# Norm, transposes and raw blocks of the first tokens set inside the preceding A22 products, first pieces in step, operands in another order

## The chip, the cores and the metric

The kernel runs on one core of a Trainium2 chip. The metric is the device time of one execution in microseconds (us). TensorE (PE) multiplies, VectorE (DVE), ScalarE (ACT) and GpSimd (POOL) do the elementwise work, and SyncE (SP) issues most DMAs.

## The reference

A trunk of two layers on x of 1 x 1024 x 1024 in float32. Cut to what matters here:

```python
def sq_relu_mlp(h, w_in, w_out):
    return jnp.square(jax.nn.relu(h @ w_in)) @ w_out

for layer in range(2):
    if layer == 0:
        x = x + rwkv7_time_mix(rmsnorm(x, rwkv_norm_g[0]), ...)   # ends in "@ w_o"
    else:
        x = x + fox_layer(rmsnorm(x, attn_norm_g[0]), w_q, ..., w_o, k_sh, v_sh, c_sh)
    x = x + sq_relu_mlp(rmsnorm(x, mlp_norm_g[layer]), w_in[layer], w_out[layer])
    if layer == 0:
        k_sh, v_sh, c_sh = shared_kv(x, kv_norm_g, kv_w, ...)     # rmsnorm(x) @ kv_w
```

w_in is 1024 x 4096, w_out 4096 x 1024, w_q and w_o 1024 x 1024, kv_w 1024 x 2064. Each large product thus begins with an RMS norm of the residual stream, which the product before it has just finished.

## The kernel before

**Products.** A float32 number is split into a high part `h` (rounded by a cast) and a low part `l` (the rest), and a product is three passes: hh, lh and hl. `split` makes the two parts with one cast and one subtraction. Large products use a scheme of seven products on the four quarters of each matrix: A11, A12, A21, A22 are the quarters of the left one, B11 to B22 those of the right one; S1 to S4 are sums on the left, T1 to T4 (code: `t1` to `t4`) sums on the right. The seven products are A11 B11, A12 B21, S1 T1, S2 T2, S3 T3, S4 B22 and A22 T4, and their sums give the four quarters of the result.

**Operands.** The normed x has to stand transposed on the right side of `mlp_in` and `stage_qkv` (q, k, v). `norm_T` scales four row tiles of x (128 x 1024 each; the first half is the first 512 tokens) by their `rstd`, and 32 transposes of 128x128 on PE bring them into PSUM; `emit_raw` copies them to SBUF as raw blocks, B11 and B21 from the first half, B12 and B22 from the second. `operands` then forms t1 to t4 and splits all of them: tiles `xh..`, `xl..` with the operand's name (xhB, xlB of B11, B21, B22; xhT, xlT of T1 to T4). The tables `ENG["m0"]`, `ENG["m1"]`, `ENG["q"]` give for each instruction a letter of the engine: v for DVE, s for ACT, p for POOL.

**Stages**, in order: mixing and recurrence of layer 0 with its w_o (to 874 us), `mlp_in` of layer 0 (16 pairs; `products(pr)` runs the seven products of one pair, 12 matmuls of 128x512 each; to about 1205), `mlp_out` of layer 0 (ends in its A22 product, 192 matmuls, to 1519), `stage_qkv` (six groups by `proj_seven`, each product 48 matmuls of 128x256; to about 1840), attention, w_o by `add_product` (to 2179), `mlp_in` of layer 1 (to about 2520) and `mlp_out` of layer 1.

**Where products and operands meet.** In `mlp_in` of layer 0 the raw blocks of the first half are made early, in the recurrence; the first two pairs' A11 and A12 stand, by a generator that stops there (`yield`), before the second transposes; afterwards each pair runs in `IN_ORDER`, the first at a higher priority. In `mlp_in` of layer 1 and `stage_qkv` `operands` begins with the first norm and transposes itself, behind the end of the product before; in q/k/v a group's A11 stands before the second transposes.

**What sets the order.** A scheduler with a simulated timeline fixes the instruction order of every engine beforehand; engines take their queues strictly in order. `tc.high_priority` moves work forward, and matmuls issued by `k.pe` keep the program's order on PE. Memory pools are opened and closed in a stack; a tile that takes the place of another waits for its last reader.

## Time and profile before

| | us |
|---|---|
| median of 3 runs | 2847.68 (2845.11 to 2850.22) |
| profiled execution, its own time | 2847.68 |
| its span | 2845.9 |
| busy: PE / DVE / ACT / POOL | 2605.9 / 2071.9 / 1282.4 / 799.2 |
| mean granted clock of PE | 0.951 |

The profiled execution is the median run; its span is 1.8 us shorter than its time. Busy is the sum over the instructions of an engine. PE's matmuls overlap in their ends, so what a stretch could have taken is read from the number of its matmuls and the distance of their starts. A wait is given with the engine and line that ended it. Granted clock 1.00 is the upper of PE's two levels (2.4 GHz), 0.50 the lower (1.2 GHz).

### The profile page before, as it was taken

To read this page: it belongs to the slowest core of one execution; us is meant where nothing else is said; L and a number is where in the kernel's file an instruction comes from. 1 tells how busy PE (TensorE), PEld (TensorE's weight loads), DVE (VectorE), ACT (ScalarE), POOL (GpSimd) and SP (SyncE) were. 2 spreads that over 40 slices of the span, in tenths; PEclk is the share of its full clock that TensorE was granted. 3 is DMA by queue.
4 is the path that set the end of the run, shared out by engine and by line. 5 is a ranking of instruction groups with operands and counts; after the bars stand their busy time and mean duration, and the time that the engine had idled before them with its cause. 6 is when DMAs were issued, how large, how long until landed. Compare 5 with 4: busy or idle time off the path is not lost. (4 is left out here: it accounts for less than half of the span.)

```text
span 2845.9 us, 46112 instructions
## 1 busy us (share of the span) xinstructions
PE 2605.9 (92%) x17922; PEld 2180.6 (77%) x17922; DVE 2071.9 (73%) x3275; ACT 1282.4 (45%) x2215; POOL 799.2 (28%) x575
## 2 busy tenths in 40 slices
PE   7998788789998999999997899899987899999999
PEld 4777677577776888788886899877876688878887
DVE  7049998777777777747776878577789877755675
ACT  6354443332234555534343434377745455543332
POOL 3056453375655000000304322233356200000030
PEclk9999889889998999999998899999998999999999
DMA  3358674565431444467561232455430344466764
GB/s 119 133 182 243 169 213 125 169 175 146 124 76 37 163 163 155 170 216 258 192 223 60 69 110 76 146 151 144 111 134 1 96 155 156 139 228 218 242 196 139
DMA packets 382315, 428.49 MB, mean 151 GB/s; under 512 B 139696, under 2 KB 259744, under 8 KB 382096
## 3 DMA queue, kind: packets, MB, share of 16 engines
q1 hardware_dynamic: 379088, 417.08, 47.0%
q0 software_dynamic: 3008, 8.47, 0.8%
q8 instruction: 141, 2.31, 0.4%
q14 instruction: 78, 0.64, 0.1%
HBM read 295.31 MB, written 130.15 MB: 150 GB/s over the span
## 5 line engine op out<-in xcount | busy, mean ns | idle before, releaser
L356 PE MATMUL mm<-oh 128*128 128x512 f32 x896 | 351.3, 392 | 9.9 <-ACT oh L702 9.9
L356 PE MATMUL mm<-ol,oh 128*128 128x512 f32 x896 | 351.3, 392 | 1.7 <-DVE ol L705 1.7
L356 PE MATMUL mm<-oh,ol 128*128 128x512 f32 x896 | 350.7, 391 | 0.0
L702 ACT CAST oh<-ra 128x1024 fp32r<-128x1024 f32 x112 | 117.8, 1054 | 354.7 <-PE mm L356 257.1
L705 DVE TENSOR_TENSOR ol<-ra,oh 128x1024 fp32r<-128x1024 f32 x112 | 142.7, 1276 | 140.5 <-ACT oh L702 140.3
L739 PE MATMUL mm<-xlT,ah 128*128 128x512 f32 x512 | 203.1, 397 | 13.1 <-DVE xlT L705 13.1
L738 PE MATMUL mm<-xhT,ah 128*128 128x512 f32 x512 | 202.5, 396 | 12.4 <-DVE xhT L704 6.4
L356 PEld LDWEIGHTS mm<-oh 128*128 128x128 f32 x896 | 169.7, 189 | 46.0 <-ACT oh L702 10.7
L356 PEld LDWEIGHTS mm<-ol,oh 128*128 128x128 f32 x896 | 169.5, 189 | 38.3 <-DVE ol L705 2.7
L740 PE MATMUL mm<-xhT,al 128*128 128x512 f32 x512 | 197.2, 395 | 0.2 <-DVE al L705 0.2
L356 PEld LDWEIGHTS mm<-oh,ol 128*128 128x128 f32 x896 | 169.6, 189 | 35.2
L702 ACT CAST ah<-w 128x512 fp32r<-128x512 f32 x125 | 77.6, 622 | 157.1 <-PE mm L739 150.3
L738 PE MATMUL mm<-xhB,ah 128*128 128x512 f32 x368 | 144.9, 394 | 0.0
L739 PE MATMUL mm<-xlB,ah 128*128 128x512 f32 x368 | 144.6, 393 | 0.0
L740 PE MATMUL mm<-xhB,al 128*128 128x512 f32 x368 | 144.5, 393 | 0.0
L1485 POOL DMA_DIRECT2D d_x<-xt x16 | 8.8, 549 | 482.7 <-DVE xt L1478 482.3
L1485 POOL DMA_DIRECT2D out_dram<-xt x16 | 8.7, 545 | 477.3 <-DVE xt L1478 477.0
L739 PEld LDWEIGHTS mm<-xlT,ah 128*128 128x128 f32 x512 | 97.8, 191 | 36.7 <-DVE xlT L705 16.4
L705 DVE TENSOR_TENSOR ol<-rb,oh 128x1024 fp32r<-128x1024 f32 x96 | 125.6, 1310 | 0.0
L738 PEld LDWEIGHTS mm<-xhT,ah 128*128 128x128 f32 x512 | 97.7, 191 | 35.3 <-ACT xhT L702 11.8
L356 PE MATMUL mm<-wl,xhT 128*128 128x256 f32 x384 | 111.2, 289 | 7.9 <-POOL wl L705 7.9
L356 PE MATMUL mm<-wh,xlT 128*128 128x256 f32 x384 | 111.7, 291 | 6.6 <-POOL xlT L705 6.6
(528 smaller groups left out, 7481.6 us busy)
## 6 DMA issues: line engine op xcount, KB each, us to landing
rb<-in_mlp_w_out_dram SPq DMA_DIRECT2D x128, 512.0 KB
ra<-d_H SPq DMA_DIRECT2D x112, 512.0 KB
w<-in_mlp_w_in_dram SPq DMA_DIRECT2D x64, 512.0 KB
d_H<-z SPq DMA_DIRECT2D x32, 1024.0 KB
d_H<-sums SPq DMA_DIRECT2D x32, 512.0 KB
raw<-in_rwkv_w_rkv_dram SPq DMA_DIRECT2D x24, 512.0 KB
d_KR<-KR SPq DMA_DIRECT2D x16, 512.0 KB
KRz<-d_KR SPq DMA_DIRECT2D x16, 512.0 KB
```

What stands on the lines that cost most here:

```text
L356: return self.tc.keep_in_program_order(self.tc.nc.tensor.matmul(*args, **kw))
L702: nc.scalar.copy(hi, src)
L705: lo_eng.tensor_tensor(lo, src, hi.bitcast(F32), op=ALU.subtract)
L738: te.matmul(out, ah, bh, start=i == 0, stop=False)
L739: te.matmul(out, ah, bl, start=False, stop=False)
L740: te.matmul(out, al, bh, start=False, stop=i == n - 1)
L1485: nc.gpsimd.dma_start(out[i * P:i * P + P, (D1, D2)[h]], d)
```

## The change

1. `operands` always gets the first half's raw blocks, made earlier by `first_half`, and a list of callbacks, `steps`, between which it makes T1 and T2 (with the second transposes), T3, B22 and T4, in this order; before, T2 came first, then T1, T4, B22, T3. t1 to t4 are written in place.
2. The first two pairs of `mlp_in` run in step, product by product in `START_ORDER`, in the pinned order of PE: A11 and A12 of pair 0, the second transposes, A11 and A12 of pair 1, S1 of both, S2 of both, and so on. Their weights' sums and splits no longer follow letters but stand on DVE and ACT. The three sums go into one tile (`bufs=1`), and an early pair needs one more addition.
3. In `mlp_out` of layer 0 a callback `mid` runs halfway through the A22 product: norm, 32 transposes and raw copies of the first half for q/k/v.
4. In `add_product` (w_o of layer 1) `mid` runs before A22: the same for `mlp_in` of layer 1. The right side's split tiles have 3 buffers, not 4.
5. In q/k/v A11 and A12 of the first group stand before the second transposes, and the pool of the weights is opened before that of the operands.

The diff, cut to this (`early` in `products` means the first two pairs; what passes `raw` and `mid` on to the stages is left out):

```diff
+    for kt in range(NK):
+        b = ("B11", "B21")[kt // 4]
+        parts(b, kt % 4, raw[kt % 4][b], (eng["Bh"][kt], eng["Bl"][kt]))
+    steps[0](X)
+
+    emit = emit_raw(k, raw, lambda b, i: tile_("T4", {"B12": "h", "B22": "l"}[b], i), gcol, eng)
     def second_parts(kt, half, tp):
         i, b = emit(kt, half, tp)
-        if b == "B22":
-            minus("t1", i, "B12", "B11", tile_("T4", "h", i))
-            minus("t2", i, "B22", "t1", tile_("B22", "h", i))
-            parts("T2", i, "t2")
-    if early:
-        for kt in range(NK):
-            first_parts(kt, 0)
-    else:
-        norm_T(k, ps_tile, xt, first_parts, lambda i: [tile_of(i)], eng, 0)
-    if mid is not None:
-        mid(X)
-    if early:
-        ss = pools["B22"].tile([P, 1], F32, name="ss")
-        row_squares(k, xt[NK - 1], last_junk, ss)
-        rsqrt_small(k, pools["B22"], k.rstd[NK - 1], ss, 1.0 / D, 1e-6)
+        r = raw[i]
+        if b == "B12":
+            minus("t1", i, r["B11"], r["B12"], r["B11"])
+            parts("T1", i, r["B11"])
+        else:
+            r["t2"] = tile_("T3", "h", i)
+            minus("t2", i, r["t2"], r["B22"], r["B11"])
+            parts("T2", i, r["t2"])
     norm_T(k, ps_tile, xt, second_parts, lambda i: [tile_("T2", "h", i - 4), tile_("B22", "l", i - 4)], eng, 1)
+    if rows_done is not None:
+        rows_done()
+    steps[1]()
     for i in R4:
-        parts("T1", i, "t1")
-    if after is not None:
-        after()
+        r = raw[i]
+        minus("t4", i, r["B21"], r["B21"], r["t2"])
+        minus("t3", i, r["B12"], r["B22"], r["B12"])
+        parts("T3", i, r["B12"])
+    steps[2]()
     for i in R4:
-        minus("t4", i, "B21", "t2", tile_("B22", "l", i))
-        minus("t3", i, "B22", "B12", t3(i))
-        parts("T4", i, "t4")
+        parts("B22", i, raw[i]["B22"])
+    steps[3]()
     for i in R4:
-        parts("B22", i, "B22")
-        parts("T3", i, "t3")
+        parts("T4", i, raw[i]["B21"])
+    steps[4]()
     return X
...
+def first_half(k, xt, raw, gcol, eng, pool, hn, ps_tile):
...
+    norm_T(k, ps_tile, xt, emit_raw(k, raw, place, gcol, eng), hn, eng, 0)
...
+START_ORDER = ["A11", "A12", "S1", "S2", "S3", "S4", "A22"]
...
-            def part(name, q, src=None):
+                nc.vector.tensor_tensor(A[dst], A[x], A[y], op=op)
+
+            def part(name, src=None):
                 S[name] = [wp.tile([P, NK // 2, P], F32R, tag=t, name=t, bufs=3) for t in ("ah", "al")]
-                es = [eng["wh"][7 * pr + q], eng["wl"][7 * pr + q]] if pr < 2 else ["s", "v"]
-                split(k, None, A[src or name], None, *(engine(k, e) for e in es), dst=S[name])
+                split(k, None, A[src or name], None, nc.scalar, nc.vector, dst=S[name])
...
-            for q, an in enumerate(IN_ORDER):
+            for an in START_ORDER if early else IN_ORDER:
...
-                    k.pe if early and pr < AHEAD and q < 2 else nc.tensor)
+                mm3(k, o, [((ah[:, i], al[:, i]), X[bn][i]) for i in range(NK // 2)], k.pe if early else nc.tensor)
...
+                    if early:
+                        yield
...
                     add(C11, U, o)
                     square(C11)
                 elif an == "S2":
                     add(U, U, o)
+                    if early:
+                        add(V, V, o)
                 elif an == "S1":
-                    V = hp.tile([P, 512], F32, tag="V", name="V", bufs=1)
                     add(V, U, o)
                 elif an == "S3":
-                    add(C22, V, o)
+                    if early:
+                        o22 = o
+                    else:
...
+                    if early:
+                        yield
+                        if pr == 0:
+                            second_place = z(1)
+                        H2 = second_place[:, pr]
+                        add(H2[:, T2], V, o22)
+                        square(H2[:, T2])
+                    C21, C22 = H2[:, T1], H2[:, T2]
...
-                    sums = [hp.tile([P, 2, 512], F32, tag="sums", name="sums") for _ in range(2)]
-                    (S1, S2), S4 = (sums[0][:, i] for i in range(2)), sums[1][:, 0]
+                    sums = hp.tile([P, 3, 512], F32, tag="sums", name="sums", bufs=1)
...
+                if early and an in ("S1", "S2", "S3"):
+                    yield
...
-        X.update(x)
+            next(gens[0])
+            if k.last_row:
+                k.last_row(hp.tile([P, 3, 512], F32, tag="sums", name="sums", bufs=1).rearrange("p a b -> p (a b)")[:, :D],
+                           xp["B22"])
+
+        def both(n):
+            for _ in range(n):
+                for g in gens[:AHEAD]:
+                    next(g)
+
+        def second():
+            next(gens[1])
+            both(1)
+        X.update(operands(k, xp, ps, xt, k.col[f"mlp_norm_g{l}"], eng, raw,
+                          [first, second, lambda: both(1), lambda: both(1), lambda: both(2)]))
         for g in gens:
...
+            if an == "A22":
+                mid(lambda i: [pool.tile([P, 512], F32, tag=t, name="hn", bufs=4) for t in ("S3", "T3")])
...
-                    h_ = op_.tile([P, 512], F32R, tag="h" + side, name="oh", bufs=4)
-                    l_ = op_.tile([P, 512], F32R, tag="l" + side, name="ol", bufs=4)
+                    h_, l_ = (op_.tile([P, 512], F32R, tag=t + side, name="o" + t, bufs=4 if side == "a" else 3) for t in "hl")
                     es = [engine(k, letters[at + side + y][4 * q + i]) for y in "hl"]
...
-        U, V = ([p["k"].tile([P, 512], F32, name=f"{n}{i}") for i in range(4)] for n in "UV")
+        UV = [p["k"].tile([P, 2, 512], F32, name=f"UV{i}") for i in range(4)]
+        U, V = ([t[:, i] for t in UV] for i in range(2))
...
+                if mid is not None and names == ("A22",) and q == KP // 2:
+                    tps = [ps.tile([P, 512], F32, tag="mm", name="tp") for _ in range(4)]
+                    mid([t.rearrange("p a b -> p (a b)") for t in UV], tps)
...
+        if number == 0 and an == "A12":
+            yield
...
+        p1 = ctx.enter_context(tc.tile_pool(name="q_1", bufs=2, reuse_waits="tile"))
         xp = operand_pools(k, ctx, "B11 B22 B21 T1 T2 T3 T4")
-        p1 = ctx.enter_context(tc.tile_pool(name="q_1", bufs=2, reuse_waits="tile"))
...
-        def first_product(x):
...
-            next(groups[0])
...
-            return t3[-1][:, i % 2]
+            step(2)
+
+        def step(n):
+            for _ in range(n):
+                next(groups[0])
...
-        operands(k, xp, ps, xt, None, t3_tile,
-                 lambda i: p1.tile([P, D], F32, tag=("wh", "wl")[i % 2], name="hn"), ENG["q"], first_product, rows_done)
+        X.update(operands(k, xp, ps, xt, None, ENG["q"], raw,
+                          [first, lambda: step(3), lambda: step(1), lambda: None, lambda: step(2)], rows_done))
```

**DVE at the end of `mlp_out` of layer 0 and the start of q/k/v.** xt is the residual, SS the sums of squares, hn (after: UV) the normed rows, w, wl the weights and their low part. Before:

```order
L1478 TENSOR_TENSOR xt_6865<-xt_6865,mm 128x512
L1478 TENSOR_TENSOR xt_7145<-xt_7145,mm 128x512
L92 TENSOR_SCALAR hn<-xt_5233,rstd_75 128x1024
...
L751 TENSOR_TENSOR SS_13683<-SS_13683 128x4
...
L92 TENSOR_SCALAR xhT_14272<-xt_6314,rstd_76 128x512
...
L704 CAST xhB_14167<-xlT_14165 128x512
L92 TENSOR_SCALAR w<-w,cols_419 128x512
L704 CAST xhB_14123<-xlT_14121 128x512
...
L704 CAST xhB_14156<-xlT_14154 128x512
L705 TENSOR_TENSOR xlB_14124<-xlT_14121,xhB_14123 128x512
L705 TENSOR_TENSOR wl<-w,wh 128x1024
```

After (xhB_14116 is a part of B21, xhB_14100 a part of B11; the xt row is the last addition of A22):

```order
L82 TENSOR_SCALAR UV_11819<-xt_5233,rstd_75 128x1024
...
L696 TENSOR_TENSOR ol<-ra,oh 128x1024
...
L695 CAST xhB_14116<-raw 128x512
L696 TENSOR_TENSOR xlB_14117<-raw,xhB_14116 128x512
...
L1500 TENSOR_TENSOR xt_7145<-xt_7145,mm 128x512
L742 TENSOR_TENSOR SS_13625<-SS_13625 128x4
...
L82 TENSOR_SCALAR xhT_14254<-xt_6314,rstd_76 128x512
...
L695 CAST xhB_14100<-raw 128x512
L696 TENSOR_TENSOR xlB_14101<-raw,xhB_14100 128x512
L82 TENSOR_SCALAR w<-w,cols_419 128x512 x6
L696 TENSOR_TENSOR wl<-w,wh 128x1024
```

The first half's norms, and B21's casts, have moved ahead of A22's last additions; B11's casts, the scaling of w and the first wl stand behind the norms of the second half, as before.

**PE at the A22 product of w_o in layer 1.** mm are products, tp the transposes; z (after: hn) holds the normed first half. Before, A22's last matmuls, the first transposes and the second ones:

```order
L1350 MATMUL mm<-oh 128x512
L1350 MATMUL mm<-oh 128x512
L1351 MATMUL mm<-ol,oh 128x512
L1352 MATMUL mm<-oh,ol 128x512
L359 MATMUL tp<-ident,z 128x128 x32
L359 MATMUL tp<-ident,xhT_21741 128x128
```

After, the last matmuls of S4, the first transposes, and A22:

```order
L1369 MATMUL mm<-ol,oh 128x512
L1370 MATMUL mm<-oh,ol 128x512
L349 MATMUL tp<-ident,hn 128x128 x32
L1368 MATMUL mm<-oh 128x512
L1369 MATMUL mm<-ol,oh 128x512
L1370 MATMUL mm<-oh,ol 128x512
```

The 32 transposes stood behind A22's 48 matmuls and stand ahead of them now.

**DVE at the start of `mlp_in` of layer 0**, from the last residual addition's neighbour on: al is the low part of a weight's split, S and w are sums of weights. Before, with the first al here further below:

```order
L586 TENSOR_TENSOR xt_7145<-xt_7145,wo 128x512
L705 TENSOR_TENSOR xlB_9138<-raw,xhB_9137 128x512
L705 TENSOR_TENSOR xlB_9146<-raw,xhB_9145 128x512
L1192 TENSOR_TENSOR S<-w_9155 128x512
L705 TENSOR_TENSOR xlB_9150<-raw,xhB_9149 128x512
L1192 TENSOR_TENSOR w_9155<-w_9153,w_9155 128x512
L101 TENSOR_SCALAR rs_v<-ss 128x1
...
L92 TENSOR_SCALAR xlB_9257<-xt_7145,rstd_76 128x512
L705 TENSOR_TENSOR al<-w_9193,ah 128x512
```

After:

```order
L576 TENSOR_TENSOR xt_7145<-xt_7145,wo 128x512
L696 TENSOR_TENSOR xlB_9137<-raw,xhB_9136 128x512
L696 TENSOR_TENSOR xlB_9145<-raw,xhB_9144 128x512
L1185 TENSOR_TENSOR S<-w_9154 128x512
L696 TENSOR_TENSOR xlB_9149<-raw,xhB_9148 128x512
L696 TENSOR_TENSOR al<-w_9152,ah 128x512
L1185 TENSOR_TENSOR w_9154<-w_9152,w_9154 128x512
L696 TENSOR_TENSOR al<-w_9152,ah 128x512
L91 TENSOR_SCALAR rs_v<-ss 128x1
L696 TENSOR_TENSOR al<-w_9320,ah 128x512
```

Three al, before on POOL or later, stand among the first ten instructions.

## Rows read from the trace of the kernel before

**Rows 1.** The page's first part: busy time, share of the span and instructions of each engine.

```profile
PE 2605.9 (92%) x17922; PEld 2180.6 (77%) x17922; DVE 2071.9 (73%) x3275; ACT 1282.4 (45%) x2215; POOL 799.2 (28%) x575
```

**Rows 2.** Stretches of time: from and to, length; then busy time and number of instructions of PE, PE's weight loads, DVE, ACT and POOL; the granted clock; the DMA engines' share, GB/s. The order is: steady part of mlp_in of layer 1; w_out's A22 product of layer 0; start of mlp_in of layer 0 (two rows); start of q/k/v and the end of its first group; start of mlp_in of layer 1 and a part of it.

```profile
2235.00:2485.00 250.00, 250.00 (x1105) 207.00 (x1104) 184.72 (x293) 128.21 (x206) 3.18 (x3) 1.00 0.46 151
1475.00:1518.80 43.80, 43.80 (x194) 35.97 (x192) 24.48 (x30) 16.85 (x27) 3.53 (x7) 1.00 0.33 109
874.00:889.00 15.00, 14.84 (x81) 12.30 (x79) 12.24 (x23) 7.97 (x16) 7.27 (x5) 1.00 0.10 27
889.00:925.00 36.00, 24.24 (x71) 17.07 (x72) 34.04 (x41) 17.02 (x32) 23.15 (x16) 0.72 0.07 19
1518.80:1600.00 81.20, 50.78 (x315) 48.24 (x315) 73.10 (x92) 31.81 (x58) 50.16 (x31) 0.75 0.19 61
1600.00:1611.30 11.30, 11.30 (x97) 11.30 (x96) 11.13 (x21) 4.47 (x9) 0.00 (x0) 1.00 0.36 135
2178.70:2230.00 51.30, 25.87 (x115) 20.47 (x115) 50.26 (x57) 28.08 (x54) 35.07 (x24) 0.78 0.04 11
2202.00:2230.00 28.00, 14.22 (x50) 9.86 (x49) 28.00 (x26) 14.51 (x26) 20.77 (x14) 0.83 0.07 19
```

**Rows 3.** Waits of PE by what ended them: us in total, times, longest. The first row is of 889 to 925, the next two of 1518.8 to 1600, the last two of 2178.7 to 2230.

```profile
PE mm L739 <- DVE xlT L705: 6.1, 4, 3.5
...
PE mm L356 <- DVE wl L705: 8.9, 1, 8.9
PE mm L356 <- POOL wl L705: 7.9, 1, 7.9
...
PE tp L359 <- DVE xhT L92: 8.4, 2, 8.1
PE mm L739 <- DVE xlT L705: 7.0, 2, 6.7
```

**Rows 4.** DVE's timeline from the end of w_out's A22 into q/k/v: start, duration of the group, line, operation, out<-in, shape, count, and in brackets the idle time before.

```profile
1514.80 0.69 DVE L1478 TENSOR_TENSOR xt<-xt,mm 128x512 f32<-128x512 f32 x1 [9.02 <-PE mm L356]
...
1519.48 2.73 DVE L92 TENSOR_SCALAR hn<-xt,rstd 128x1024 f32<-128x1024 f32 x4
...
1528.65 1.67 DVE L92 TENSOR_SCALAR xlB<-xt,rstd 128x512 f32<-128x512 f32 x4
...
1530.23 0.75 DVE L704 CAST xhB<-xlT 128x512 fp32r<-128x512 f32 x2
...
1541.40 1.21 DVE L705 TENSOR_TENSOR wl<-w,wh 128x1024 fp32r<-128x1024 f32 x1
...
1543.47 4.01 DVE L92 TENSOR_SCALAR w<-w,cols 128x512 f32<-128x512 f32 x2
...
1561.12 1.75 DVE L1107 TENSOR_TENSOR t<-xhT,xlT 128x512 f32<-128x512 f32 x1
```

**Rows 5.** PE's timeline there: the last matmul of A22, the start of q/k/v's A11, the second transposes.

```profile
1518.45 0.39 PE L356 MATMUL mm<-oh,ol 128*128 128x512 f32 x1
...
1542.67 0.58 PE L356 MATMUL mm<-wl,xhB 128*128 128x256 f32 x1 [8.94 <-DVE wl L705]
...
1550.87 1.91 PE L359 MATMUL tp<-ident,xhT 128*128 128x128 f32 x16
1552.61 1.91 PE L359 MATMUL tp<-ident,xlB 128*128 128x128 f32 x16
```

**Rows 6.** POOL's groups of instructions in 1518 to 1600: count, busy time, mean ns of one, idle time before.

```profile
L705 POOL TENSOR_TENSOR xlT<-xhT,xhT 128x512 fp32r<-128x512 f32 x4 | 6.8, 1718 | 0.0
...
L705 POOL TENSOR_TENSOR wl<-w,wh 128x1024 fp32r<-128x1024 f32 x2 | 5.0, 2476 | 0.0
```

**Rows 7.** Timeline at the start of mlp_in of layer 0, of POOL, DVE and PE: the first two al, the last residual addition, the first matmul of the first pair, the second transposes.

```profile
870.84 2.89 POOL L705 TENSOR_TENSOR al<-w,ah 128x512 fp32r<-128x512 f32 x2
...
874.72 0.68 DVE L586 TENSOR_TENSOR xt<-xt,wo 128x512 f32<-128x512 f32 x1
...
874.04 0.40 PE L356 MATMUL mm<-xhB,ah 128*128 128x512 f32 x1
...
885.19 1.91 PE L359 MATMUL tp<-ident,xhT 128*128 128x128 f32 x16
886.93 1.91 PE L359 MATMUL tp<-ident,xlB 128*128 128x128 f32 x16
```

**Rows 8.** Timeline at the end of w_o and the start of mlp_in of layer 1, of DVE and PE: S4's additions, sums of squares, the end of rstd, the first half's norms (z), the last matmul of S4 and a later one, the first transposes, the second ones, and a matmul near the end of the first two pairs' work.

```profile
2170.27 2.47 DVE L1363 TENSOR_TENSOR xt<-xt,mm 128x512 f32<-128x512 f32 x4
...
2174.10 0.16 DVE L751 TENSOR_TENSOR SS<-SS 128x4 f32<-128x4 f32 x1
...
2175.57 1.27 DVE L107 TENSOR_TENSOR rstd<-rstd,rs_t 128x4 f32<-128x4 f32 x1
2176.88 5.75 DVE L92 TENSOR_SCALAR z<-xt,rstd 128x1024 f32<-128x1024 f32 x4
...
2168.75 0.39 PE L1352 MATMUL mm<-oh,ol 128*128 128x512 f32 x1
...
2182.68 5.05 PE L359 MATMUL tp<-ident,z 128*128 128x128 f32 x29 [0.22 <-DVE z L92]
...
2199.84 2.13 PE L359 MATMUL tp<-ident,xlB 128*128 128x128 f32 x16
...
2258.76 0.39 PE L738 MATMUL mm<-xhT,ah 128*128 128x512 f32 x1
```

More of the change, by code (lines that the diff above doesn't have):

```diff
@@ L1101, in parts @@
         X[name][i] = tuple(tile_(name, part, i, F32R) for part in "hl")
[L1102 removed]
+        split(k, None, src, None, *(engine(k, e) for e in es or (eng[name + "h"][i], eng[name + "l"][i])),
               dst=X[name][i])
[L1105 to L1109 removed]
@@ L1110, in operands, with minus @@
-    early = raw is not None
-    raw = raw or [{} for _ in R4]
-    emit = emit_raw(k, raw, lambda b, i: tile_(*rest[b], i), gcol, eng)
-    def first_parts(kt, half, tp=None):
-        i, b = emit(kt, half, tp) if tp is not None else (kt % 4, ("B11", "B21")[kt // 4])
-        parts(b, i, b, (eng["Bh"][kt], eng["Bl"][kt]))
+    def minus(name, i, dst, x, y):
+        engine(k, eng[name][i]).tensor_tensor(dst, x, y, op=ALU.subtract)
+    for kt in range(NK):
+        b = ("B11", "B21")[kt // 4]
+        parts(b, kt % 4, raw[kt % 4][b], (eng["Bh"][kt], eng["Bl"][kt]))
```

155 lines of the change are left out of this document (72 added, 83 removed).

## The prediction

> **What bounds the kernel now.** The page comes first [rows 1]: TensorE (PE) is busy for 92% of the span and no other engine for more than 73%, so only time in which PE stands still, or runs at the lower of its two clock levels, can be won. The table of stretches says where that is [rows 2]. In the steady part of mlp_in, 1105 matmuls of 128x512 take 250 us at granted clock 1.00: 0.226 us each, nothing lost. Inside w_out's A22 product 194 matmuls take 43.8 us: again nothing lost. I use 0.226 us for a 128x512 matmul, 0.109 for a transpose (16 in the 1.74 us between the starts of two groups, [rows 5]) and 0.117 for a 128x256 matmul (97 in 11.3 us, [rows 2]). At the lower level each takes about twice that: the granted clock is 0.72 to 0.78 over the three stretches below, each with pauses before it falls. A stretch loses its length minus its matmuls at these prices:
>
> - T1, start of mlp_in 0 (889 to 925): 71 matmuls, 16.0 us of work in 36.0, 20.0 lost.
> - T2, w_out to q/k/v (1518.8 to 1600): 315 instructions, 64 of them transposes: 7.0 + 251 x 0.117 = 36.4 of 81.2, 44.8 lost.
> - T3, w_o to mlp_in 1 (2178.7 to 2230): 115 instructions, 64 of them transposes: 7.0 + 51 x 0.226 = 18.5 of 51.3, 32.8 lost.
>
> The waits of PE name what ends these pauses [rows 3]: splits and scaled copies on DVE, POOL and ACT, that is, the making of operands. DVE is busy for 90 to 98% of them [rows 2]. So in all three places two limits lie one behind the other: when the chain norm, transposes, split begins, and how fast DVE and POOL get through the splits. The change moves the first; it moves little of the second.
>
> **T2, part by part.** Added inside A22: four norms of 128x1024 on DVE (2.73 us for four, [rows 4]), 32 transposes (32 x 0.109 = 3.5 us of PE) and their copies on ACT. DVE is busy 24.5 of 43.8 us there and ACT 16.9 [rows 2], and DVE stands idle 9.0 us before the last adds [rows 4], so the copies and norms are hidden; PE's 3.5 us are not, since PE was full. Price: +3.5. Were that cover gone, the norms would add up to 2.7.
>
> Taken away behind A22: first norm, first transposes, and part of the wait for the first splits. Before, PE finishes A22 at 1518.84 (its last matmul starts at 1518.45) and starts A11 in earnest at 1542.67 [rows 5], 23.8 us later. If all of this vanished, T2 would gain 23.8 - 3.5 = 20.3. But the order on DVE says otherwise: only B21's casts stand ahead of A22's last adds. B11's four casts, two of its subtractions, six scalings of w and the first wl stand behind the adds, the rstd of the second half and seven norms, although their inputs are ready. I add up what now stands between A22's end and A11: adds 0.6, rstd 2.1 (it took 2.7 from 2174.10 to 2176.84 beside POOL's work, [rows 8]), seven norms 2.9 (0.42 each, [rows 4]), four casts 1.5 (0.37 each, [rows 4]), two subtractions 2.4 (1.2 each, between 0.69 alone and 1.75 beside POOL, [rows 4]), six scalings 3.8 (0.63 each, nearer to the 0.42 of a norm of that shape than to the 2.0 that two took beside POOL, [rows 4]), wl 1.2 [rows 4]: 14.5 us. A11 thus starts 18.0 us after the old end of A22 instead of 23.8.
>
> Then A11 and A12 run together (96 matmuls: 8.4 us for the first 48, from 1542.67 on at half clock at first, and 5.6 for the rest, with 0.3 between) and the second transposes follow (3.5): they end 14.5 + 14.3 + 3.5 = 32.3 after A22, or 35.8 after its old end; before, they ended at 1554.5, 35.7 behind it [rows 5]. What is late next is S1: its four xlT stand on POOL behind two subtractions, a 128x1024 wl (2.5 to 2.8) and other splits of 1.7 each [rows 6]; nine in all take 1 x 2.6 + 8 x 1.7 = 16 us, with ACT's copies ahead of them 18. S1 (48 matmuls, 5.7) ends about 56 after A22, and S2, S3, A22 and S4 at the same step, the last at 80, hence 83.5 by the old clock, where before the group was through at 1611.3, 92.5 after. The rest has fewer gaps: wl's 7.9 us wait ahead of S2 [rows 3] falls into S1's. **T2: -9.0**, with -20 (all hidden) and -2 (A11's 5.8 us less the 3.5 that A22 pays) as ends. I take the middle since the DVE rows that I added are those of the static order.
>
> **T1.** Norm and transposes of the first half were already early, so only the order changes. Before, two pairs' A11 and A12 (48 matmuls) ran without a gap from 874.04 with both al made by POOL beforehand [rows 7]. Now al is on DVE, fifth behind the last residual add: 875.4 + 5 x 0.6 = 878.4 [rows 7], so PE stands 4.4 us, then some 5 us at half clock cost another 2. After the transposes (889.2, nearly as before) 24 matmuls of pair 1 remain as cover for the operands of S1, whose last xlT comes at about 901.6; 7 us are lost there, some 8 more until the second pair's S2 has its al (eleven DVE rows later). In sum 4.4 + 2 + 7 + 8 = 21.4 against 20.4 (20.0, and 0.4 from 874 to 889, where 49 matmuls and 32 transposes are 14.6 of 15.0). In step, each new operand feeds 24 matmuls instead of 12, which is why the later steps, from S3 on, wait no more. **T1: +1**, from -4 to +5. One buffer for the three sums makes DVE wait for the first pair's DMA, some 4 us; DVE is idle for 65 of 250 us in such a steady stretch [rows 2], so nothing. The two extra adds (1.2) hide there too.
>
> **T3.** The norm and transposes now stand ahead of w_o's A22 on PE, but their norm needs the sums that S4's adds close. Before, S4's adds end at 2172.7, rstd at 2176.8, and the first norm begins at 2176.9 [rows 8]; A22 ran meanwhile. Now PE idles from S4's end (2169.0) to 2177.2, 8.2 us, transposes cost 5.2, A22's 48 matmuls (10.9) end at 2193.3; before, both were done at 2187.7. So this part alone is 5.6 us late. In return B11 and B21 are split while A22 runs: A11 and A12 of pair 0 follow at once (5.4), the second transposes wait for rstd and norm of the second half (2201 to 2205.5; before to 2201.97), pair 1's A11 and A12 run to 2211, S1 waits for POOL's last xlT to 2216.7, S1 of pair 1 to 2225 and S2 of pair 1 to 2234, with the matmuls between. Lost: 8.2 + 1.7 + 3.3 + 5.7 + 5.6 + 3.6 = 28.1; before 34.1 from 2169 to 2258.9, where the 168 matmuls of the first two pairs are done (89.9 minus 48 + 168 matmuls and 64 transposes, 55.8). **T3: -6**, from -12 to +4. One less buffer on the b side may lengthen PE's waits of w_o; from nothing to 2 us, in the range.
>
> **Sum.** -9 + 1 - 6 = -14 on the profiled execution of 2847.68 us (span 2845.9), which is also the median: **2834 us**. Weights' forms that POOL made in the first two pairs are now DVE's: 21 of 128x512. A POOL one takes 1.4 us [rows 7]. Beside POOL a DVE one takes 1.75 instead of 0.69 [rows 4], 1.06 more in 1.7 us of POOL; so 1.4 us of POOL cost DVE some 0.9, and making it itself costs 0.6. I count that as nothing; at most 21 x 0.3 = 6 us, half on the path.
>
> **Rivals.**
> 1. All of it hides: B11's splits slip into A22's shadow in time, T2 gains 20, and the pairs in step halve the loss of T1 (-8) and T3 (-14): 2847.7 - 42 = 2806. For it: DVE is idle in A22 (9.0 us). Against: the static order of DVE, and DVE at 28.0 of 28.0 us in 2202 to 2230. Chance 0.12.
> 2. Each microsecond of POOL costs DVE a whole one. Then taking 21 forms from POOL gives back 21 x (1.4 - 0.6) = 17 us of DVE in T1 and T3, some 13 on the path: 2821. Against: 1.06 extra in 1.7, as above. Chance 0.06. The Trainium skill, SBUF — State Buffer, section "Who interferes with whom", states it as an exclusive lock, in which one of a VectorE instruction with two SBUF inputs and a GpSimd one that reads SBUF blocks fully; by that rule this rival's time would hold, while the trace shows a partial toll.
> 3. Work conserved: DVE gets through the same splits by the same time, A11 starts sooner and S1 waits longer. T2 -2, T1 +2, T3 -1: 2847. For it: DVE at 28.0 of 28.0. Chance 0.18.
> 4. Slower: the norm set ahead of w_o's A22 decides. PE stands 8.2 us and starts A22 at half clock (2.5), T3's second half starts 5.6 late; if rstd of the second half then ends DVE's chain as late as A22 (2193.3) plus its old 17 us to the second transposes' end, T3 becomes +8, T1's al +4.4, T2 -4: 2856. It decides once the second transposes end after 2210. Chance 0.12.
>
> **How the numbers follow.** Forecast 0.52 (2822 to 2842). The range reaches over rivals 2, 3 and half of 4 and leaves out 1: 2812 to 2855. A measurement of this kernel tells 0.2%, 5.7 us, from no change: faster means below 2842.0, slower above 2853.4. Faster 0.52 + 0.12 + 0.06 = 0.70; same 0.18; slower 0.12.
>
> **What would show it.** A11 of q/k/v 12 to 17 us after A22's last matmul; S1 waiting on POOL's xlT; a pause of some 8 us on PE ahead of w_o's transposes; 4 us after wo at the start of mlp_in 0; steady stretches still at 0.226 a matmul. A11 directly behind A22 would speak for rival 1, second transposes of mlp_in 1 ending behind 2210 for rival 4. The forecast is wrong, too, if the norms and copies set into w_out's A22 make PE wait there: 43.8 us should become 47.3.

## The result, and the profile after

The changed kernel takes 2861.83 us (median of 4 runs, 2858.19 to 2863.78) where the kernel before took 2847.24 in the same session: ratio 1.0049, 95% interval 1.0032 to 1.0066. It is slower, by 14.6 us, outside the forecast range. The profiled execution took 2858.19 us, its span 2856.5.

The page's first part, after; [rows 1] answers to it:

```profile
PE 2598.7 (91%) x17922; PEld 2175.6 (76%) x17922; DVE 2064.6 (72%) x3297; ACT 1280.4 (45%) x2223; POOL 772.3 (27%) x553
```

PE's busy time is 7.2 us less than before in a span 10.6 us longer. So PE waits more. Where it does is seen from stage lengths (in us), taken from PE's timeline: each runs from one named matmul to another, since absolute times shift.

| stage | before | after | change | forecast |
|---|---|---|---|---|
| T1: wo's last matmul to the 168th of mlp_in 0 | 62.5 | 67.1 | +4.6 | +1 |
| T2: mlp_in 0's last matmul to the last of q/k/v's first group | 406.7 | 406.1 | -0.6 | -9 |
| q/k/v's last matmul to the first score matmul | 5.5 | 19.0 | +13.5 | none |
| attention, first score to w_o's first matmul | 242.5 | 239.1 | -3.4 | none |
| T3: w_o's first matmul to the 168th of mlp_in 1 | 176.1 | 175.4 | -0.7 | -6 |
| from there to the end | 580.4 | 581.5 | +1.1 | 0 |

They add up to +14.5; in this one profile the stage before T1 ended 4.0 earlier, which leaves the span's +10.6. That stage is hardly changed, and its end moves by ten microseconds between the profiles of this study (below), so totals are compared by medians and stages by their lengths.

The stretches, after; columns as in [rows 2]. They are w_out's A22; q/k/v's first group, from A22's end on; T1's part from 889 on; w_o up to S4's last matmul; steady mlp_in of layer 1:

```profile
1475.00:1522.30 47.30, 46.71 (x223) 38.85 (x222) 31.64 (x40) 20.14 (x33) 5.94 (x8) 1.00 0.41 142
...
1523.30:1611.20 87.90, 54.15 (x378) 52.11 (x378) 71.47 (x100) 32.15 (x58) 49.06 (x29) 0.77 0.16 52
...
889.00:925.00 36.00, 23.16 (x81) 17.07 (x80) 34.37 (x44) 14.60 (x26) 15.48 (x10) 0.81 0.11 30
...
2093.00:2184.10 91.10, 72.88 (x291) 56.88 (x289) 81.88 (x87) 33.00 (x67) 61.63 (x39) 0.93 0.29 99
...
2275.00:2525.00 250.00, 249.49 (x1101) 206.42 (x1100) 184.87 (x291) 128.24 (x210) 0.00 (x0) 1.00 0.48 155
```

The first row holds the 32 transposes, and PE is busy for 46.71 of its 47.30 us at granted clock 1.00: the norms and copies set into A22 do not make PE wait, as forecast. The steady part is untouched. The start of q/k/v is still at 0.77 (0.78 before, from 1518.8 to 1611.3).

PE's waits, after, answering to [rows 3]: T1 (866 to 940), T2 (1523 to 1612), the start of attention (1820 to 1860), and w_o with the start of mlp_in 1 (2093 to 2272; L1368 and L1369 are w_o's):

```profile
PE mm L346 <- DVE al L696: 8.8, 3, 4.5
PE mm L346 <- DVE xlT L696: 6.1, 1, 6.1
PE mm L346 <- ACT ah L693: 2.5, 2, 1.4
...
PE mm L346 <- ACT wh L693: 18.9, 2, 12.9
PE mm L346 <- POOL xlT L696: 6.9, 2, 4.5
PE mm L346 <- ACT xhT L693: 5.7, 1, 5.7
...
PE s L346 <- DVE Q L1845: 19.2, 2, 18.7
...
PE mm L1369 <- DVE ol L696: 14.1, 5, 7.8
PE mm L346 <- DVE al L696: 8.6, 2, 7.2
PE tp L349 <- DVE hn L82: 5.3, 1, 5.3
...
PE mm L1369 <- POOL ol L696: 3.2, 1, 3.2
```

The largest of them, 18.7 us ahead of the first score matmul, is in a stage that the prediction never speaks of. SyncE's DMA queue shows how it arises. Before (start, duration of the group, line, DMA, count; d_v takes q/k/v's last results, raw are attention's first K and Q tiles):

```profile
1815.59 1.11 SPq L1803 DMA_DIRECT2D raw<-d_k  x2
1824.49 0.37 SPq L1642 DMA_DIRECT2D d_v<-C  x1
1824.96 1.44 SPq L1803 DMA_DIRECT2D raw<-d_k  x2
...
1830.18 0.37 SPq L1642 DMA_DIRECT2D d_v<-C  x1
1830.65 2.28 SPq L1803 DMA_DIRECT2D raw<-d_r  x2
```

After:

```profile
1824.52 11.81 SPq L1666 DMA_DIRECT2D d_v<-C  x3
1836.37 2.77 SPq L1826 DMA_DIRECT2D raw<-d_k  x4
1839.25 2.17 SPq L1710 DMA_DIRECT2D aw<-in_attn_w_o_dram  x4
1845.25 3.38 SPq L1826 DMA_DIRECT2D raw<-d_r  x4
```

K's first load stood ahead of the last three stores; now it stands behind them. Each store waits for its C, which DVE writes as the last products end, and the rows show nothing passing a store that waits: the three hold the queue from 1824.52 to 1836.33, and the first load goes out 20.8 us later. Q's (d_r) goes out 14.6 later, for its two tiles are those of K, which must be split first. The order comes from memory: opening the pool of the weights ahead of the operand pools moves both in SBUF, and by the addresses in the compiled program (no trace shows them) attention's raw tiles now lie on U and V of q/k/v's last group, in use to its end, where they lay on parts of B21 before.

The Trainium skill, DMA: Bandwidth & Descriptors, section "Issuing engines are not separate DMA queues", says that issuing from several engines saves only the time of issuing itself. Issuing a store takes 0.37 us in the rows before, so by that sentence alone the queue of three stores would not matter; the rows after show that stores that wait hold up the loads behind them by far more.

### The profile page after: what moved, and what is told of

The parts are those of the page before. It is cut to its first block, busy times and chain, and to the rows that moved or that the text cites. A ratio compares the mean times of both kernels' runs of the same rounds, so it can differ in the third digit from the quotient of the medians.

```text
span 2856.5 us, 45992 instructions
## 1 busy us (share of the span) xinstructions
PE 2598.7 (91%) x17922; PEld 2175.6 (76%) x17922; DVE 2064.6 (72%) x3297; ACT 1280.4 (45%) x2223; POOL 772.3 (27%) x553
## 5 line engine op out<-in xcount | busy, mean ns | idle before, releaser
L729 PE MATMUL mm<-xhT,ah 128*128 128x512 f32 x448 | 175.0, 391 | 0.6 <-ACT ah L693 0.5
L730 PE MATMUL mm<-xlT,ah 128*128 128x512 f32 x448 | 174.8, 390 | 0.0
L731 PE MATMUL mm<-xhT,al 128*128 128x512 f32 x448 | 169.9, 390 | 0.0
L731 PE MATMUL mm<-xhB,al 128*128 128x512 f32 x336 | 131.4, 391 | 0.0
L730 PE MATMUL mm<-xlB,ah 128*128 128x512 f32 x336 | 131.3, 391 | 0.0
L729 PE MATMUL mm<-xhB,ah 128*128 128x512 f32 x336 | 131.3, 391 | 0.0
L346 PE MATMUL mm<-wh,xhT 128*128 128x256 f32 x384 | 112.8, 294 | 11.7 <-ACT wh L693 6.0
L1195 ACT ACTIVATE z<-z 128x512 f32<-128x512 f32 x128 | 80.8, 632 | 92.7 <-DVE z L1192 92.2
```

What stands on the lines that cost most here:

```text
L346: return self.tc.keep_in_program_order(self.tc.nc.tensor.matmul(*args, **kw))
L729: te.matmul(out, ah, bh, start=i == 0, stop=False)
L730: te.matmul(out, ah, bl, start=False, stop=False)
L731: te.matmul(out, al, bh, start=False, stop=i == n - 1)
L1195: nc.scalar.activation(x, x, AF.Relu)
```

## Experiments

The theory: the start of attention is two thirds of the loss (13.5 us less the 3.4 by which attention is shorter), and the single moved line of the pool order makes it. The rivals: w_o's pause ahead of its transposes, the weights' low parts moved to DVE in T1, or a lag that attention regains anyway. Ratios are to the kernel before, run beside each kernel on the same chip; 0.001 is 2.8 us. The changed kernel stands at 1.0049. Columns are stages of the table above, in us.

| kernel | ratio, 95% interval | T1 | T2 | gap | attention | T3 |
|---|---|---|---|---|---|---|
| before + pool order | 1.0049 [1.0036, 1.0061] | 62.5 | 408.7 | 19.1 | 240.0 | 179.8 |
| after, stores on another queue | 1.0034 [1.0021, 1.0047] | 68.7 | 406.6 | 11.3 | 239.7 | 176.5 |
| after, w_o's norm behind A22 | 1.0037 [1.0025, 1.0049] | 68.4 | 406.5 | 19.1 | 238.6 | 170.0 |
| after, al on POOL | 1.0067 [1.0052, 1.0081] | 65.0 | 406.1 | 19.1 | 237.9 | 178.7 |
| after, B11 placed early | 1.0029 [1.0018, 1.0040] | 66.5 | 400.1 | 19.1 | 234.1 | 177.9 |
| after, T3's parts off POOL | 1.0029 [1.0019, 1.0039] | 66.4 | 403.7 | 19.1 | 240.9 | 175.6 |
| after, K's loads on ScalarE's queue | 1.0036 [1.0023, 1.0049] | 67.0 | 406.0 | 16.6 | 238.2 | 175.1 |
| five of these edits together | 0.9993 [0.9983, 1.0002] | 66.1 | 397.6 | 15.8 | 236.5 | 171.4 |
| after, first loads free | 0.9995 [0.9984, 1.0006] | 67.8 | 406.3 | 4.6 | 239.0 | 176.1 |
| first loads free, with three edits | 0.9936 [0.9921, 0.9951] | 66.6 | 398.7 | 5.0 | 242.3 | 170.1 |
| before + three buffers in w_o | 1.0015 [1.0003, 1.0028] | 62.5 | 406.2 | 4.9 | 239.3 | 180.1 |
| before + weights' parts on DVE | 1.0024 [1.0014, 1.0034] | 64.6 | 408.5 | 5.6 | 240.2 | 180.1 |

**The pool order alone, in the kernel before.**

```diff
+        p1 = ctx.enter_context(tc.tile_pool(name="q_1", bufs=2, reuse_waits="tile"))
         xp = operand_pools(k, ctx, "B11 B22 B21 T1 T2 T3 T4")
-        p1 = ctx.enter_context(tc.tile_pool(name="q_1", bufs=2, reuse_waits="tile"))
```

> Starts from the kernel before; one edit: in q/k/v the pool of the weights is opened ahead of the operands' pools, as in the change. Theory A (this one line moves the tiles raw of attention onto tiles that q/k/v uses to its end, and the loads behind the last stores): first score matmul 10 to 15 us later against the end of q/k/v's matmuls than in the kernel before (5.5 us there), the whole 7 to 11 us slower than before, 2854 to 2858. Rival B (the line is harmless, weights come earlier): 2843 to 2848, first score matmul 5 to 7 us behind q/k/v.

SyncE's queue and PE's wait in that run:

```profile
1823.97 11.80 SPq L1642 DMA_DIRECT2D d_v<-C  x3
1835.82 2.80 SPq L1803 DMA_DIRECT2D raw<-d_k  x4
...
1844.71 3.38 SPq L1803 DMA_DIRECT2D raw<-d_r  x4
```

```profile
PE s L356 <- DVE Q L1822: 19.3, 2, 18.9
```

The gap is 19.1, and the time rises by 0.49%: one moved line, with no instruction added, makes the whole of the gap and costs as much as the whole change does. The rest of the change is thus worth nothing in sum, as far as two intervals tell that each reach 4 to 5 us to either side.

**The stores on GpSimd's queue, the first loads pinned ahead.** For the last group the d_v stores go out on POOL's queue; attention's K pool is opened first, and the first loads keep the program's order ahead of the loads of w_o.

```diff
-                nc.sync.dma_start(dst[512 * th:512 * th + 512, f:f + 256].rearrange("(t p) e -> p t e", p=P),
+                q = nc.gpsimd if f0 else nc.sync
+                q.dma_start(dst[512 * th:512 * th + 512, f:f + 256].rearrange("(t p) e -> p t e", p=P),
...
-                    nc.sync.dma_start(t[r], src[p * P + j * 64:p * P + j * 64 + 64, :])
+                    (tc.keep_in_program_order if p == 0 else lambda x: x)(
+                        nc.sync.dma_start(t[r], src[p * P + j * 64:p * P + j * 64 + 64, :]))
```

> Starts from the changed kernel; only the order of loads at the start of attention is altered: the last group's d_v stores go to GpSimd's queue, the tiles raw, K, Q are opened first among attention's pools, and the first K and Q loads and the w_o weight loads are kept in this order on SyncE's queue. Theory A (the late Q load, which stands behind stores that wait for q/k/v's last sums, costs the time): the first score matmul comes at 1836 to 1842 us instead of 1853.9, and the whole is 8 to 11 us faster than the changed kernel, about 2851. Rival B (attention is late for another reason, the load order only marks it): first score matmul not before 1850, time within 2 us of the changed kernel, 2860 to 2864.

Only part of it came: gap 11.3, first score at 1850.1, and the ratio falls by 0.0015, some 4 us. GpSimd's timeline shows the new stop:

```profile
1828.62 0.79 POOL L1667 DMA_DIRECT2D d_v<-C  x1 [2.33 <-DVE C L1605]
1834.31 0.75 POOL L1667 DMA_DIRECT2D d_v<-C  x1 [4.91 <-DVE C L1605]
1840.06 0.75 POOL L1667 DMA_DIRECT2D d_v<-C  x1 [5.00 <-DVE C L1605]
1840.83 4.64 POOL L1840 TENSOR_TENSOR K<-raw,K 128x1024 fp32r<-128x1024 f32 x2
```

K was there by 1829.8, when ACT begins to cast it, but its split is POOL's too and now stands behind the moved stores; Q's loads wait for that split. The waiting stores hold up GpSimd's queue as they held up SyncE's.

**K's first loads on ScalarE's queue.** The K pool opened first as above, and for the first pair `nc.scalar.dma_start` in place of `nc.sync.dma_start`.

> Starts from the changed kernel; attention's tiles raw, K, Q are opened first and the first K and Q loads are issued by ScalarE's queue, nothing else. Theory A (in the earlier attempt the K splits on GpSimd stood behind the stores that were moved to its queue; the queue is the whole cause): first score matmul 4 to 7 us behind q/k/v's last matmul instead of 19, the whole 9 to 12 us faster than the changed kernel. Rival B (part of the delay is in the K and Q splits themselves): 9 to 13 us behind.

Both numbers missed: gap 16.6. On ACT K's loads stand behind its last casts of the weights, which wait for PE; they go out at 1829.85. Q's go out at 1845.45, although K's second split ends at 1841.6: in the trace they wait for the semaphore by which the last d_v store, issued on SyncE's queue at 1842.1, reports its landing. So here, too, the last stores set Q's start, from another queue.

**w_o's norm and transposes behind A22.** The call of `mid` moved to the end of `add_product`.

```diff
-            if an == "A22":
-                mid(lambda i: [pool.tile([P, 512], F32, tag=t, name="hn", bufs=4) for t in ("S3", "T3")])
...
+    mid(lambda i: [pool.tile([P, 512], F32, tag=t, name="hn", bufs=4) for t in ("S3", "T3")])
```

> Starts from the changed kernel; the norm, transposes and raw blocks in w_o of layer 1 stand behind the A22 product instead of ahead of it; all else, also three buffers on the right side, stays. Theory A (the pause ahead of the transposes and A22 at the lower clock cost as much as the early splits give back): within 3 us of the changed kernel. Rival B (ahead of A22 it is a gain, as in the forecast): 4 to 10 us slower than the changed kernel. Rival C (the pause decides): 4 to 8 us faster.

T3 falls from 175.4 to 170.0 and the ratio by 0.0012, some 3 us. The total alone, between theories A and C and with an interval that overlaps the changed kernel's, does not decide; the stage does. With this code T3 is 170.0 to 171.4 in three kernels, with the changed kernel's 175.1 to 177.9 in six. The pause that A22 used to hide is the dearer side: the raw blocks made early gain less than the 5.3 us of PE's wait `tp <- DVE hn`.

**al of A11 and A12 on GpSimd**, in the first two pairs of both layers.

```diff
-                split(k, None, A[src or name], None, nc.scalar, nc.vector, dst=S[name])
+                es = (nc.scalar, nc.gpsimd) if early and name in ("A11", "A12") else (nc.scalar, nc.vector)
+                split(k, None, A[src or name], None, *es, dst=S[name])
```

> Starts from the changed kernel; the low parts of the weights of A11 and A12 of the first two pairs are made by GpSimd, in both layers, as the first two were before. Theory A (PE stands at the start of mlp_in of layer 0 because al is behind VectorE's other work): the waits of 1.1 and 3.6 us ahead of A11 go, 3 to 5 us faster than the changed kernel. Rival B (the end of the first two pairs is set by the splits of T1 and T2 on VectorE and GpSimd): the pause moves to S1, time within 1.5 us.

T1 gains 2.1, PE's waits on al there fall from 8.8 to 4.8, but T3 does not gain and the total is, if anything, longer. The gain in T1 is barely clear of the spread: with the changed kernel's code T1 is 66.4 to 68.7 in eight kernels, and 66.1 in the one with five edits, which has the same four al on POOL. The change's four al are worth some 2 us of T1 at most, not all of its 4.6.

**B11's tiles placed early.** In q/k/v B11's casts stand behind the norms because their tiles lie on those of mlp_out's normed rows; another order of the pools frees them, and the first group's weights are scaled on ScalarE. Two things are changed at once, and what each gives is not told apart.

```diff
-        "wl": "vpvpvpvvvvpvpv", "wf": "pvvvvpvv", "wg": "vvvpvvsvvvvvssss"},
+        "wl": "vpvpvpvvvvpvpv", "wf": "pvvvvpvv", "wg": "ssssssssvvvvssss"},
...
-        xp = operand_pools(k, ctx, "B11 B22 B21 T1 T2 T3 T4")
+        xp = operand_pools(k, ctx, "B22 B11 B21 T1 T2 T3 T4")
```

> Starts from the changed kernel. In q/k/v the operand pools are opened as B22, B11, B21 instead of B11, B22, B21, so that B11's parts lie where w_out's raw tiles end early and not where its norm rows and sums of squares lie; and the first group's eight scalings of w are ACT's. Theory A (memory that was still in use and VectorE's queue held A11 back, not the number of splits): A11's first matmul 7 to 10 us after A22's end instead of 13.1, A12's end 22 to 25 us after it instead of 27.9, the first group done 3 to 7 us earlier against the end of mlp_in of layer 0. Rival B (VectorE and GpSimd get through the splits by the same time): A11 earlier, S1 waits longer, group 1 within 1.5 us.

PE's waits in 1520 to 1612:

```profile
PE mm L346 <- ACT wh L693: 13.8, 2, 7.7
PE mm L346 <- POOL xlT L696: 6.9, 2, 4.5
PE mm L346 <- ACT xhT L693: 5.8, 1, 5.8
```

The wait ahead of A11 falls from 12.9 to 7.7, the later ones stay as they were, and T2 falls by 6.0: what the head wins reaches the group's end in full. The steps behind it do not eat it up. The ratio falls by 0.0020, 5.7 us.

**T3's parts off GpSimd in q/k/v.** Letters `"T3h": "spvv"` to `"ssvv"`, `"T3l": "vpvp"` to `"vvvv"`.

> Starts from the changed kernel; in q/k/v the parts of T3 that GpSimd made are made by VectorE and ScalarE. Theory A (t1 to t4 are written in place, so T4's casts on ScalarE wait for T3's parts, and the cast of S3's weights stands behind them; that is the pause of 6.0 us ahead of S3): the pause falls below 2 us, group 1 ends 3 to 6 us earlier. Rival B (S3 is late for its weights alone, in two buffers): pause 4 to 6 us, time within 1.5 us.

T2 falls by 2.4. PE's wait on ACT's wh, in two pauses as after, falls from 18.9 to 16.5 with the first still 12.9, so the pause ahead of S3 is 3.6 in place of 6.0: the splits on POOL are a part of it and not the whole, and both numbers lie between the two theories. The ratio falls by 0.0020, 5.7 us; for what that exceeds T2's 2.4 no stage accounts.

**Five edits together**: B11 early, T3 off POOL, K's loads on ScalarE's queue, w_o's norm behind A22, and al of A11 and A12 on POOL in layer 0 alone.

> The changed kernel with the edits of the two runs on q/k/v, the attention loads on ScalarE's queue, w_o's norm and transposes behind A22, and the low parts of the first two pairs' A11 and A12 on GpSimd in layer 0 only. If the losses are separate and add: 3 for the first pairs, 6 for w_o, 13 less 3 for attention, 4 to 10 for q/k/v from the changed kernel's 2862, that is 2833 to 2842, 3 to 12 us faster than the kernel before. If VectorE's work is conserved from stage to stage and gains in one come back in the next: 2845 to 2852.

T2 is 397.6, 9.1 shorter than before, T3 4.7 shorter; the gap, 10.3 longer, and T1's +3.6 take all of it back. The median of 2844.8 lies between the two expectations and is no different from the kernel before.

**The first loads freed of every wait.** To the second experiment (stores on GpSimd's queue) are added tiles of their own for Q's first loads, and the first pair's K splits on DVE:

```diff
-        raws = [kp.tile([P, T], F32, tag="raw", name="raw") for _ in range(2)]
+        raws = [kp.tile([P, T], F32, tag=t, name="raw") for t in ("K11", "K10", "raw", "raw")]
...
-                nc.gpsimd.tensor_tensor(K2[j], t, K1[j].bitcast(F32), op=ALU.subtract)
+                (nc.gpsimd if p else nc.vector).tensor_tensor(K2[j], t, K1[j].bitcast(F32), op=ALU.subtract)
```

> The changed kernel with every wait taken from attention's first loads: its K and Q tiles lie where the raw blocks and the weights were (dead early), the loads stand ahead of the last d_v stores, Q's two loads have tiles of their own instead of K's, and the first pair's K splits run on VectorE. Theory A (the late start of attention is two thirds of the loss): the gap from q/k/v's last matmul to the first score matmul falls from 19.0 us to 4-7, attention gives back some 3 of the 13 (as its span in the changed kernel is 3.4 shorter than before), and the time falls by 8-12 us, to 2850-2854. Rival B (the gap is only where a lag shows that attention's vector work has anyway): the gap closes and attention's span grows by as much, and the time stays within 3 us of the changed kernel's 2862.

SyncE's queue and PE's wait there:

```profile
1818.87 4.43 SPq L1826 DMA_DIRECT2D raw<-d_k  x4
1823.34 3.72 SPq L1826 DMA_DIRECT2D raw<-d_r  x4
```

```profile
PE s L346 <- DVE Q L1845: 4.3, 1, 4.3
```

The gap is 4.6, and attention's span stays at 239.0, so nothing had been given back. The 3.4 us by which attention is shorter after the change are no more than the spread between profiles: with the code of the kernel before it took 242.5 in the first and 239.3, 240.0 and 240.2 in three others. The ratio falls by 0.0054, some 15 us, a little more than expected. With attention's start repaired the changed kernel is level with the one before. The five edits of this kernel act on one chain and were not taken apart further.

**First loads free, with three of the edits**: B11 early, T3 off POOL, w_o's norm behind A22.

> The same, with first-group weights scaled on ScalarE, B11's tiles off the norm's rows, T3's parts off GpSimd, and the norm of the next MLP behind w_o's A22 (all pieces run before, without the one that moved al to GpSimd). Theory A: terms add; 2844.8 with the four pieces and a gap of 15.8 becomes 2833-2838 with a gap of 4-7, ratio to the kernel before 0.994-0.997: the forecast of 2834 is met once the start of attention is paid back. Rival B: 2843-2847, no difference from the kernel before.

2831.22 us (median of 6) against 2846.28, and the ratio, 0.9936, is a little below the expected band: the terms add up (0.9995 less 0.0020, 0.0020 and 0.0012 is 0.9943). This version beats both kernels.

**Three buffers in w_o, in the kernel before.** `bufs=4 if side == "a" else 3` for the split tiles, all else as before.

> The kernel before, with nothing changed but the right side's split tiles in w_o, which have 3 buffers instead of 4 as in the changed kernel. In the changed kernel w_o's part up to S4's last matmul is 91.1 us long against 86.1 before. Theory A (the missing buffer makes w_o's splits late): this part becomes 90-92 us, with waits of PE on the low parts made by VectorE and GpSimd of 14-18 us in place of 13.9 on both engines, and the time rises by 4-5 us, 2850-2852. Rival B (the normed rows' place and the moved work in it do that, not the buffers): 86-87 us and no change of time.

w_o, first to last matmul, is 100.8 us in place of 95.6, +5.2; up to S4's last matmul it is 90.1 in place of 84.5 (not 86.1: S4 ends earlier than the text above has it, see T3 below). The time rises by 0.15%, some 4 us. PE's waits up to S4:

```profile
PE mm L1350 <- ACT oh L702: 6.9, 1, 6.9
PE mm L1351 <- DVE ol L705: 6.4, 4, 3.2
PE mm L1351 <- POOL ol L705: 2.5, 1, 2.5
```

They sum to 15.8 against 13.9 before: the buffer decides, and only part of its price is PE standing still.

**The weights' parts on DVE, in the kernel before.** For the first two pairs in layer 0 `"wh"` all s, `"wl"` and `"wf"` all v.

> The kernel before, with nothing changed but the letters of the first two pairs' weights in the MLP of layer 0: all their high parts on ScalarE, all low parts and sums on VectorE, as in the changed kernel, while the order of the products stays as before. T1, from wo's last matmul to the 168th matmul of the MLP, is 62.5 us before and 67.1 in the changed kernel. Theory A (the weights' place decides): 66-68 us, with waits on VectorE's al of some 4-9 us, and 4-5 us on the total, 2850-2852. Rival B (the order in step decides): 62-63.5, no wait on al over 2 us, and no change of time.

T1 is 64.6, between the two theories. PE's waits in 866 to 940, of which two on al are new:

```profile
PE mm L356 <- DVE al L705: 3.3, 1, 3.3
...
PE mm L740 <- DVE al L705: 1.3, 1, 1.3
```

The weights' place is worth some 2 us of T1's 4.6, as the run with al on POOL said from the other side; the rest belongs to the order in step or to the two together. The total rises by 0.24%, 6.8 us, more than T1 does; where the rest arises is not shown (T2 and T3 are longer in this profile, by no more than their spread).

## Why the prediction was wrong, point by point

**The step that failed** is one that the prediction did not take. It costs each part of the change in T1, T2 and T3 and says of the moved line of the pool order nothing at all: the line stands in the sum at zero, without a reason. That line is the loss: alone it costs 0.49%, undone in effect it gives back 0.54%. In the profiles it is 13.5 of the 28.5 us between the forecast of -14 and the stages' +14.5; most of the others are 8.4 in T2, 5.3 in T3 and 3.6 in T1, treated below. A pool's place in the stack sets what a later tile lies on, that sets what its load waits for, and that sets where the load stands in an in-order queue. The prediction reads the order of DVE, POOL and PE, and never that of SyncE's queue; there the rows differ, raw ahead of d_v before and behind it after.

**T2: -9 forecast, -0.6 measured.** The head was right. PE from A22's last matmul on, after: the first matmul of A11, the second transposes, the first of S1, the first of S3:

```profile
1523.34 0.39 PE L346 MATMUL mm<-oh,ol 128*128 128x512 f32 x1
...
1536.67 0.58 PE L346 MATMUL mm<-wh,xhB 128*128 128x256 f32 x1 [12.94 <-ACT wh L693]
...
1553.31 1.91 PE L349 MATMUL tp<-ident,xlB 128*128 128x128 f32 x16
...
1560.94 0.58 PE L346 MATMUL mm<-wh,xhT 128*128 128x256 f32 x1 [5.72 <-ACT xhT L693]
...
1589.49 0.58 PE L346 MATMUL mm<-wh,xhT 128*128 128x256 f32 x1 [5.97 <-ACT wh L693]
```

A22's last matmul starts at 1523.34 and has its 0.23; A11 starts 13.1 behind that end (forecast 14.5), and the second transposes end 31.6 behind it (32.3). S1 waits for POOL's xlT, as forecast, and for ACT's xhT ahead of it, and S2 ends 60 behind A22, 2 us sooner than the forecast's steps would have it. The group's end was wrong: at 1611.2 it comes 87.6 behind A22, not 80. S2, S3, A22 and S4 were priced "at the same step"; but ahead of S3 PE waits 5.97 for a wh, and the start of that stretch is at half clock (0.58 us a matmul, granted clock 0.55 from 1589.4 to 1597.0). ACT's rows show where that wh stands:

```profile
1587.39 0.62 ACT L693 CAST xhT<-raw 128x512 fp32r<-128x512 f32 x1 [2.11 <-POOL xlT L696]
...
1588.39 1.99 ACT L693 CAST wh<-w 128x1024 fp32r<-128x1024 f32 x2
```

It comes behind casts of T4 (here raw), and those wait for POOL's xlT of T3, because t1 to t4 are now written in place. The experiment with T3 off POOL takes 2.4 of it away. The transposes in A22 cost 4.3 (mlp_out of layer 0, 314.0 to 318.3), forecast 3.5. So -9 should have been -0.6: +7.6 at the group's end, +0.8 at the transposes. (The -0.6 itself is of one pair of profiles: with the code of the kernel before T2 was 406.2, 406.7 and 408.5.) DVE also took 0.88 for a scaling of w, not 0.63:

```profile
1529.83 1.43 DVE L695 CAST xhB<-raw 128x512 fp32r<-128x512 f32 x4
...
1532.37 5.26 DVE L82 TENSOR_SCALAR w<-w,cols 128x512 f32<-128x512 f32 x6
```

Rival 1's gain in T2 lay in these casts of B11 and these scalings: placed early, or moved to ScalarE, they give 6.0 (B11 placed early), not the 20 of its price, with 7.7 of waiting left ahead of A11.

**T1: +1 forecast, +4.6 measured.** The pauses were right: 4.4 forecast up to the first al's matmuls and 4.64 measured (1.05 of it for ACT's ah), 7 and 6.1 at S1, 8 and 6.65 up to S2; 17.4 in all by the waits. The rest of the loss was wrong. 168 matmuls and 32 transposes are 41.5 us at full clock, so 25.6 of the 67.1 are lost. The 8.2 in which PE does not wait go with the lower clock (0.81 from 889 to 925), where the forecast put 2. Before, 21.0 are lost, 11.9 of them in waits by the same view. The change added 5.5 of waiting. The term that was mis-sized is the clock's: the forecast's 21.4 for after, with 2 of it, was held against a measured 20.4 for before, which had all of it.

**T3: -6 forecast, -0.7 measured.** The prediction counts from S4's end at 2169.0, and its row for that, of 2168.75 [rows 8], is not S4's last matmul. A22's first matmuls, which wait for their own splits, start at 2167.38 and 2167.60, and from there to 2175 no matmul signals the end of a product. S4's last is this one:

```profile
2167.15 0.39 PE L1352 MATMUL mm<-oh,ol 128*128 128x512 f32 x1
```

S4's adds start at 2170.27 because DVE has splits for A22 ahead of them. From S4's last matmul to the 168th of mlp_in 1 the stage after is as forecast, 84.3 us (83.9); before it is 91.6, not 89.9. The gain there, 7.3, is more than the 6: in four kernels with the old code this part took 89.9 to 95.7, in six with the new one 84.3 to 85.4. The pause ahead of the transposes is there, 5.3 instead of 8.2:

```profile
2189.59 5.95 PE L349 MATMUL tp<-ident,hn 128*128 128x128 f32 x32 [5.31 <-DVE hn L82]
...
2219.70 2.52 PE L349 MATMUL tp<-ident,xlB 128*128 128x128 f32 x16
```

The loss is ahead of it: w_o up to S4's last matmul is 91.1 instead of 84.5, 6.6 longer. "One less buffer ... from nothing to 2 us" was the mis-sized term; alone it measures 5.6 up to S4 and 5.2 over all of w_o. T3 is also a noisy stage: with nothing in it changed it was 176.1, 179.8 and 180.1, so the change may gain up to 4 more there than the one pair of profiles says.

**The rivals.** Rival 4 named the norm ahead of w_o's A22, with a point of decision: second transposes behind 2210. They end at about 2222.2, on the old clock 2212.1 (w_o starts 10.1 later after the change), so the point was passed, by w_o's 6.6 alone; but T3 did not become +8, for from there to the 168th matmul took 46.3 instead of 57.0. Its total of 2856 came nearest by luck, not by its mechanism. Rival 3, work conserved, came near in its total for the rest of the change (with attention's start repaired the ratio is 0.9995), but its mechanism did not show: B11 placed early shortens T2 by all that A11 gains.

Rival 2 got nothing: POOL's busy time fell by 26.9 us, DVE's by 7.3 and no stage by 13. The argument against it, a partial toll of 1.06 us, misreads [rows 4], however. Where a POOL subtraction of 128x512 and one on DVE meet, the rows are these (POOL, then DVE, in the kernel before):

```profile
1557.19 1.75 POOL L1107 TENSOR_TENSOR t<-xhT,xlT 128x512 f32<-128x512 f32 x1
1556.01 3.49 DVE L1107 TENSOR_TENSOR xhT<-xlT,xlT 128x512 f32<-128x512 f32 x2
```

The second of the two on DVE starts at 1557.7, while POOL's runs; POOL's ends at 1558.94, DVE's at 1559.50. In that trace 84 DVE instructions of this shape with both inputs in SBUF that start while a POOL one runs take over 0.75 us, and each of them ends 0.55 us after POOL's: it waits that instruction out, and the 1.06 of [rows 4] comes from the 1.2 us that were left of it. This agrees with the exclusive lock that the Trainium skill, SBUF — State Buffer, section "Who interferes with whom", states. Why the work taken off POOL brought no stage forward even so is not shown.

## What to carry to other kernels

A pool that is opened elsewhere moves every tile above it. Before such a line is priced at nothing, read each DMA queue's order at the next stage's start: which loads come behind a store or a cast that waits for the last results. Stores that wait held up SyncE's queue and GpSimd's alike (gaps of 19.0 and 11.3), and loads moved to ScalarE's queue still waited (16.6). The gap was short where the loads' tiles were free early: 5.5 in the kernel before, with its stores on SyncE's queue, and 4.6 with tiles of their own. And measure a change by the lengths of all stages, also of those that it doesn't name: the five edits together shortened T2 and T3 by 14 us, and a gap in a third place hid it.

## What had not been expected

The mixing and recurrence stage, which no experiment touches, ended between 868.0 and 878.7 us after the start of the span in fourteen profiles. T3 spread over 4 us in three kernels in which it is the same (176.1 to 180.1), attention over 3.2 in four (239.3 to 242.5), T1 over 2.3 in eight (66.4 to 68.7). A single profile can't carry a difference of 3 us between such stages. T2, 406.0 to 406.6 in six kernels with the changed code there, can; with the old code it was 406.2, 406.7 and 408.5.
